# A hybrid attention, recurrence and mixture-of-experts block on one core: scores a step ahead, earlier splits, own tiles for raw weights, a gate spread by DMA

## Chip, cores and metric

One core of a Trainium2 chip runs the whole kernel as one launch. The metric is device time in microseconds (us), the median of several runs. TensorE is called PE, VectorE DVE, ScalarE ACT, GpSimd POOL and SyncE SP, as in the profile.

## The reference, cut to what matters

One layer on 512 latent tokens of width 1024 and 256 context tokens, all in float32. Two branches read the same projection; their outputs are lifted, gated and projected; a mixture of experts follows (32 experts, two per token).

```python
h  = ada_rmsnorm(x, g_mix, sh1, sc1);  hc = ada_rmsnorm(ctx, g_mix, mod_c[0], mod_c[1])
proj = h @ w_in;  proj_c = hc @ w_in[:, :CTX_COLS]
o_att = neighbourhood_attention(q, k, v, k_c, v_c, rpb)       # 8 heads of 64, window 8 x 16, plus all context keys
o_lru = (h_f + h_b) * gelu(proj[..., LG_OFF:...])             # conv, then scans in both directions, 1024 channels
y = sigmoid(proj_ga) * (o_att @ w_up_attn) + sigmoid(proj_gb) * (o_lru @ w_up_lru)
x = x + ga1 * (y @ w_out)
h2 = ada_rmsnorm(x, g_ffn, sh2, sc2)
x = x + ga2 * hier_moe(h2, ...)                               # top group, top-2 experts, SwiGLU 1024 -> 512 -> 1024
return rms(x) * g_final
```

## The kernel before

Most products are made exact to float32 by splitting both factors into a high and a low part and adding three products (`mm3`, L47). `wsplit` (L52) does this for a block of weights: SP loads the raw block, ACT copies it to a high part, DVE subtracts to get the low part. Raw and low tiles take turns in one ring of four buffers, `wlo`; the high tiles have a ring of three, `whi`. `next_weights` (L322) keeps two blocks in hand in the order that `weights_in_order` (L299) writes out.

A planner with a simulated clock (`schedule_with_timeline_sim`) lays out each engine's queue; `high_priority` and `issue_after` steer it, and `queued()` with `tail` ties the products of PE to the order of the program. Each engine then works through its queue in order.

The stages are:

- A prologue normalises x and the context, makes the first modulation and the values of attention.
- Four head pairs, j = 0 to 3 (L635). A pair is `keys` (L363), `queries` (L379), two of `lru_x` (L453, a projection of 512 latent and 256 context columns and a convolution), then `attend` (L394). `attend` goes over four blocks b of 128 queries: scores of two heads into the two banks of `at`, softmax on DVE (L416) and ACT (L418, L420), transposes (L429), products with the values (L440). Between these it calls `between(n)`, which runs n steps of the generator `others(j)` (L615): gate projections (`gate`, L521, result to DRAM), recurrences (`lru_g`, L474) and GeLU gates (`lru_o`, L510). A projection has three steps, `lru_g` four.
- `mod2` (L530) makes the second modulation on the side: 4 groups of 8 steps, each a load on POOL's queue and a multiply-add on DVE (L544). At a group's end ones-products sum it in a bank of `at` (L547), and a bias row comes over POOL's queue (L553). `others` calls one step after each of its eight parts. The relative bias of attention is loaded on POOL's queue too (L601).
- After the last pair `high` (L570) splits the four attention and eight recurrent outputs into high and low parts; `lift` (L578) multiplies them with `ua` and `ul`, two lifts of attention ahead of the first of the recurrence. SBUF that the pairs held comes free, and loads of x2, of w_out and of the first expert weights start there.
- The output projection and the router (`outp`, L750), with the tokens of the first expert pair gathered by one-hot products (L819) after 40 small products (L857).
- Sixteen expert pairs (L1110). Each reads 12 blocks of 1 MB: 8 for gate and up (`gu`, L1078), 4 for down (`down`, L1088). A ring of 22 tiles and two early ones hold the blocks that SP loads ahead (L908). `act` (L972) is the SiLU product and its transposes; `combine` (L988) scales by the routing weight and `ga2` and adds to x2 by one-hot products. `rows` (L932) gathers the next pair's tokens on POOL's queue. At pair 0, ahead of its last gate and up block, the two early tiles are closed, their place goes to the tiles of `act` and `combine`, and `broadcast` (L1032) loads the one row of `ga2` on SP's queue and spreads it over 128 partitions by products with ones and copies (L1037, L1038).

Of the kernel before, what the change touches and what calls it, by code (L numbers as in the profile page):

```python
# [9 lines left out]
F32 = mybir.dt.float32  # L10
# [27 lines left out]
def tile_block(ctx: ExitStack, tc: tile.TileContext, A, out):  # L38
# [13 lines left out]
    def wsplit(src, shape):  # L52

        n = shape[0] * shape[1]
        raw = ws.tile([128, 1024], F32, name="wlo", bufs=4)
        SP.dma_start(raw[:, :n], src)
        lo = ws.tile([128, 1024], F32R, name="wlo", bufs=4)
        hi = ws.tile([128, 1024], F32R, name="whi", bufs=3)
        S.copy(hi[:, :n], raw[:, :n])  # L59
        V.tensor_tensor(lo[:, :n], raw[:, :n], hi[:, :n].bitcast(F32), op=ALU.subtract)  # L60
        pat = "p (a b) -> p a b"
        return hi[:, :n].rearrange(pat, a=shape[0]), lo[:, :n].rearrange(pat, a=shape[0])

    tail = [None]
# [47 lines left out]
    ob = [op.tile([128, T], F32, name="ob", bufs=13) for _ in range(12)]  # L112
    olru = ob[4:]
# [185 lines left out]
    def weights_in_order():  # L299
        for j in range(4):  # L300
# [4 lines left out]
            for i in range(2):  # L305
                yield A["wcol"][24 + 4 * j + 2 * i], (NK, 128)
                if j < 3:
                    yield A["wcol"][24 + 4 * j + 2 * i + 1], (NK, 128)
                    yield A["wcol"][16 + 2 * j + i], (NK, 128)
                else:  # L310
                    yield A["wcol"][16 + 2 * j + i], (NK, 128)
                    yield A["wcol"][24 + 4 * j + 2 * i + 1], (NK, 128)
# [81 lines left out]
    def attend(j, kr, kx, qr, qp, between):  # L394

        po = ps.tile([128, 4, 128], F32, name="po")
        for b in range(4):
            w0 = WIN[b]
            scs = [ps.tile([128, 512], F32, name="at", bufs=2) for z in range(2)]
            q = slice(128 * b, 128 * b + 128)  # L400
            Ps, pts = [], []
            with tc.high_priority():

                with queued():
                    for c0, qs, ks in ((0, qr, kr[:, :, 8 * w0:8 * w0 + 256]), (256, qp, kx)):
                        for n, (a, h) in enumerate(((0, 0), (1, 0), (0, 1))):
                            for z, hs in enumerate(HALF):
                                cs = slice(256 - c0, 512 - c0) if z else slice(c0, c0 + 256)
                                m = PE.matmul(scs[z][:, cs], qs[hs, a, q], ks[hs, h, :], start=(n == 0), stop=(n == 2))
                tail[0] = m.ins  # L410
                for z in range(2):
                    sc = scs[z]
                    P = p1.tile([128, 512], F32, name="P", bufs=2)
                    st = p1.tile([128, 8], F32, name="st", bufs=4)

                    V.tensor_tensor_reduce(out=sc, in0=sc, in1=bias[z], scale=-1.0, scalar=3.0e38, op0=ALU.add,  # L416
                                           op1=ALU.min, accum_out=st[:, 0:1])
                    S.activation(P, sc, AF.Exp, bias=st[:, 0:1], scale=-1.0, accum_out=st[:, 3:4])  # L418
                    V.reciprocal(st[:, 4:5], st[:, 3:4])
                    S.activation(P, P, AF.Copy, scale=st[:, 4:5])  # L420
                    Ps.append(P)
            load_bias(j, b + 1)
            between(3)
            for z in range(2):
# [8 lines left out]
                between(1)  # L433
            with tc.high_priority():
# [100 lines left out]
    def mod2_g(g):  # L535
# [11 lines left out]
        pm = ps.tile([128, 256], F32, name="at", bufs=2)  # L547
# [10 lines left out]
        else:  # L558
            mt = ps.tile([128, 2, 128], F32, name="pt")
# [50 lines left out]
    kq = {}  # L610
    for step in (keys(0, kq), queries(0, kq), lru_x(0), lru_x(1)):
        for _ in step:
            pass

    def others(j):  # L615

        for i in range(2):
            c = 2 * j + i
            yield from gate(4 * j + 2 * i)
            next(m2s, None)  # L620
            yield from lru_g(c)
            next(m2s, None)
            if c < 7:
                lru_w(c + 1)
            if j < 3:
                yield from gate(4 * j + 2 * i + 1)
                next(m2s, None)
                yield from lru_o(c)
            else:
                yield from lru_o(c)  # L630
                next(m2s, None)
                yield from gate(4 * j + 2 * i + 1)
            next(m2s, None)

    for j in range(4):  # L635
        rest = others(j)
# [5 lines left out]
        attend(j, **kq, between=between)  # L642
        for _ in rest:
            pass
        if j < 3:
            kq = {}
# [788 lines left out]
```

## Time and profile before

| | us |
|---|---|
| median of 3 runs | 1072.51 (1071.69 to 1074.51) |
| the profiled execution | 1068.22 |
| its span, first to last instruction | 1066.5 |
| PE busy | 1003.0 (94%) |
| DVE busy | 562.5 (53%) |
| ACT busy | 428.9 (40%) |
| moved by DMA | 293.89 MB, mean 276 GB/s |

A busy share is a mean over the whole span. The share in each stage, and what an engine waits for there, has to be read stage by stage. PE's granted clock has two levels here, 1.0 for 2.4 GHz and 0.5 for 1.2 GHz.

### The profile page before, as it was taken

What the parts mean: (1) busy time and instruction counts of PE and PEld (TensorE: products, weight loads), DVE (VectorE), ACT (ScalarE), POOL (GpSimd) and SP (SyncE); (2) the same over time, 40 slices, a digit from 0 to 9 for tenths busy, and PEclk for the clock granted to TensorE, in tenths of its full rate; (3) what the DMA queues carried; (4) which work ended last, traced back from release to release, by engine and by line L of the source; (5) the groups of instructions that cost most, each with busy time, mean ns of one, the idle gap of its engine ahead of it and who ended that gap; (6) DMA issues with size and microseconds to landing.
All of it is one profiled execution on the core that took longest, in us unless ns stands there. A gap on an engine that the chain in (4) does not pass through costs nothing.

```text
span 1066.5 us, 13848 instructions
## 1 busy us (share of the span) xinstructions
PE 1003.0 (94%) x5196; PEld 614.3 (58%) x5196; DVE 562.5 (53%) x1150; ACT 428.9 (40%) x762; POOL 95.1 (9%) x159
## 2 busy tenths in 40 slices
PE   8998989989998999889999799999999999989995
PEld 7787768767876866568787434444444344333332
DVE  5678559657865965767448423333333353322234
ACT  4334784776488377724122122222222222212204
POOL 0021011101101100211001300000000000000001
PEclk9999999999999999989999989999999999999998
DMA  9575235324423622385787979999999999999992
GB/s 372 194 253 173 95 135 175 116 98 158 138 91 119 205 92 79 114 315 191 263 328 279 385 274 420 420 421 420 420 420 421 420 420 419 421 420 421 422 398 97
DMA packets 59034, 293.89 MB, mean 276 GB/s; under 512 B 8705, under 2 KB 9241, under 8 KB 33364
## 3 DMA queue, kind: packets, MB, share of 16 engines
q1 hardware_dynamic: 43636, 252.45, 59.5%
q0 software_dynamic: 11856, 34.22, 9.6%
q10 hardware_dynamic: 3472, 6.30, 1.6%
q8 instruction: 42, 0.69, 0.3%
q14 instruction: 28, 0.23, 0.1%
HBM read 287.24 MB, written 9.65 MB: 278 GB/s over the span
## 4 chain that ended last, share of the span: by engine, by line
PE 58%; DMA 22%; ACT 9%; DVE 7%; issue 2%; SPq 0%; ACTq 0%; DVEq 0%
DMA w<-in_ew 16%; PE g L1084 13%; PE y L1097 7%; PE pj L48 7%; PE pj L49 6%; PE pj L50 6%; DMA wlo<-in_wcol 3%; PE pj L489 2%; PE pc L1003 2%; PE pc L1004 2%; DVE wlo L60 1%; PE po L759 1%; DMA wlo<-in_ua 1%; PE po L761 1%; PE po L760 1%
## 5 line engine op out<-in xcount | busy, mean ns | idle before, releaser
L1084 PE MATMUL g<-w,xg 128*64 128x512 f32 x1024 | 232.5, 598 | 5.5 <-DMA w<-in_ew 4.9
L1084 PEld LDWEIGHTS g<-w,xg 128*64 128x64 f32 x1024 | 68.3, 136 | 139.9 <-issue 119.7
L48 PE MATMUL pj<-hh,whi 128*128 128x512 f32 x320 | 131.5, 411 | 0.1
L49 PE MATMUL pj<-hl,whi 128*128 128x512 f32 x320 | 127.1, 397 | 0.0
L50 PE MATMUL pj<-hh,wlo 128*128 128x512 f32 x320 | 126.8, 396 | 0.0
L1097 PE MATMUL y<-w,hT 128*64 128x512 f32 x512 | 115.7, 601 | 5.8 <-DMA w<-in_ew 5.2
L947 ACT ACTIVATE xg<-pc,sh2col,s2col 128x128 f32<-128x128 f32 x120 | 45.1, 459 | 153.1 <-PE pc L944 153.1
L977 DVE TENSOR_TENSOR hm<-hm,g 128x512 f32<-128x512 f32 x16 | 11.0, 688 | 179.1 <-PE g L1084 165.8
L60 DVE TENSOR_TENSOR wlo<-wlo,whi 128x1024 fp32r<-128x1024 f32 (+1 forms) x60 | 69.0, 1151 | 46.0 <-ACT whi L59 45.8
L59 ACT CAST whi<-wlo 128x1024 fp32r<-128x1024 f32 (+1 forms) x60 | 59.4, 991 | 78.3 <-DMA wlo<-in_wcol 26.3
L1097 PEld LDWEIGHTS y<-w,hT 128*64 128x64 f32 x512 | 35.3, 139 | 82.8 <-issue 60.6
L994 DVE SCALAR_TENSOR_TENSOR hm<-y,stok,ga 128x512 f32<-128x512 f32 x31 | 23.3, 751 | 110.6 <-PE y L1097 110.6
L1006 DVE TENSOR_TENSOR x<-x,pc 128x512 f32<-128x512 f32 x122 | 75.6, 680 | 6.3 <-PE pc L1004 6.3
L995 ACT CAST y_h<-hm 128x512 fp32r<-128x512 f32 x31 | 19.2, 620 | 131.8 <-DVE hm L994 71.5
L48 PEld LDWEIGHTS pj<-hh,whi 128*128 128x128 f32 x320 | 60.4, 189 | 17.6 <-ACT tr L491 2.9
L50 PEld LDWEIGHTS pj<-hh,wlo 128*128 128x128 f32 x320 | 60.4, 189 | 14.7
L49 PEld LDWEIGHTS pj<-hl,whi 128*128 128x128 f32 x320 | 60.5, 189 | 12.1
L1003 PE MATMUL pc<-y_h,ot 128*128 128x512 f32 x122 | 51.3, 421 | 0.3 <-ACT xg L947 0.3
L489 PE MATMUL pj<-xc,ga 128*128 128x256 f32 (+1 forms) x128 | 49.7, 516 | 0.0
L934 POOL DMA_INDIRECT xr<-nd,toki x15 | 16.7, 1113 | 354.2 <-PE pc L981 271.3
L1004 PE MATMUL pc<-y_l,ot 128*128 128x512 f32 x122 | 48.0, 393 | 0.0
L49 PE MATMUL pj<-ob,whi 128*128 128x512 f32 x96 | 39.3, 409 | 5.2 <-DVE ob L575 5.2
(372 smaller groups left out, 1668.8 us busy)
## 6 DMA issues: line engine op xcount, KB each, us to landing
w<-in_ew SPq DMA_DIRECT2D x191, 1024.0 KB, 20.1
wlo<-in_wcol SPq DMA_DIRECT2D x40, 512.0 KB, 3.6
m<-in_wm POOLq DMA_DIRECT2D x32, 512.0 KB, 4.1
wm<-in_wm SPq DMA_DIRECT2D x8, 1024.0 KB, 11.8
bias<-in_rpb POOLq DMA_DIRECT2D x32, 128.0 KB, 2.4
gd<-ga ACTq DMA_DIRECT2D x16, 256.0 KB, 3.7
wlo<-in_ul SPq DMA_DIRECT2D x8, 512.0 KB, 3.4
ga<-gd POOLq DMA_DIRECT2D x16, 256.0 KB, 3.6
```

Source lines behind the costliest of these rows:

```text
L48: PE.matmul(o, wh, hh, start=start, stop=False)
L49: PE.matmul(o, wh, hl, start=False, stop=False)
L50: return PE.matmul(o, wl, hh, start=False, stop=stop)
L59: S.copy(hi[:, :n], raw[:, :n])
L60: V.tensor_tensor(lo[:, :n], raw[:, :n], hi[:, :n].bitcast(F32), op=ALU.subtract)
L489: m = PE.matmul(pg[:, 0:n], lw[:, 128 * w:128 * w + 128], xc[:, s0:s0 + n], start=True, stop=True)
L947: S.activation(xg[z][:, k % 4, :], pg[:, k % 4, :], AF.Identity, bias=sh2col[:, k:k + 1], scale=s2col[:, k:k + 1])
L1003: PE.matmul(pc, ot[:, i, :], y_h, start=True, stop=False)
L1004: m = PE.matmul(pc, ot[:, i, :], y_l, start=False, stop=True)
L1006: V.tensor_add(x2[:, i, ns], x2[:, i, ns], pc)
L1084: m = PE.matmul(pgu[pr][v][64 * e:64 * e + 64, :], xg[pr][k // 4][:, k % 4, 64 * e:64 * e + 64], w[:, v, e, :], start=(k == 0), stop=(k == ...
L1097: m = PE.matmul(py[64 * e:64 * e + 64, :], hT[:, k, 64 * e:64 * e + 64], w[:, k % 2, e, :], start=(k == 0), stop=(k == 3))
```

## The change

- **Scores a step ahead.** `attend` is cut in two. `scores(j, b)` holds the scores, the softmax and the load of the next bias; `attend` calls `scores(j, b + 1)` before the transposes of block b. Block 0's scores stand in `start(j)`, between the two `lru_x`. `P` has three buffers. The calls of `between` are 2, 1, 2, 1 instead of 3, 1, 1, 1.
- **Second modulation.** Its sums and transposes use the ring `pj` (four banks, those of the projections) instead of `at` and `pt`; `others` calls up to 12 steps per pair.
- **Branch outputs.** The attention output is split straight from PSUM into `oatt`. In pair 3 the order of `others` is new (both recurrences early, two gates last), and `high(c)` splits the recurrent outputs while the pair runs, into the tiles of the context's `hh` and `hl`, whose pool now lives as long as the lifts.
- **Raw weights.** While the lifts run, `wsplit` puts raw blocks into two tiles of their own.
- **Small steps later.** The router's constants and two index steps are issued after lift 10.
- **Experts.** `ga2` is spread by one DMA on POOL's queue. At pair 0, 34 products of 128 x 128 stand between the gate and up products and the activation.

```diff
-        raw = ws.tile([128, 1024], F32, name="wlo", bufs=4)
+        raw = (wraw[0] or ws).tile([128, 1024], F32, name="wraw" if wraw[0] else "wlo", bufs=2 if wraw[0] else 4)
...
+    hcp = R.enter_context(pool("hTc", "right"))
     r1 = R.enter_context(ExitStack())
-    hcp = r1.enter_context(pool("hTc", "right"))
...
-    ob = [op.tile([128, T], F32, name="ob", bufs=13) for _ in range(12)]
-    olru = ob[4:]
+    oatt = [[op.tile([128, T], F32R, name=f"oa{z}{j}") for z in range(2)] for j in range(4)]
+    olru = [op.tile([128, T], F32, name="ob", bufs=9) for _ in range(8)]
...
-    def attend(j, kr, kx, qr, qp, between):
+    def scores(j, b, kr, kx, qr, qp):
...
+                P = p1.tile([128, 512], F32, name="P", bufs=3)
...
+        load_bias(j, b + 1)
+        return Ps
+
+    def attend(j, kq, Ps, between):
         po = ps.tile([128, 4, 128], F32, name="po")
         for b in range(4):
...
-            load_bias(j, b + 1)
-            between(3)
+            between(2)
+            ahead_ = scores(j, b + 1, **kq) if b < 3 else None
+            pts = []
             for z in range(2):
...
-                between(1)
+                between(1 + z)
...
                 if b == 3:
-                    V.tensor_copy(ob[j].rearrange("p (r b c) -> p b r c", b=4, c=16),
-                                  po.rearrange("p b (r c) -> p b r c", c=16))
+                    pat = "p (r b c) -> p b r c"
+                    src = po.rearrange("p b (r c) -> p b r c", c=16)
+                    h, l = (o.rearrange(pat, b=4, c=16) for o in oatt[j])
+                    S.copy(h, src)
+                    V.tensor_sub(l, src, h.bitcast(F32))
             between(1)
+            Ps = ahead_
...
-        pm = ps.tile([128, 256], F32, name="at", bufs=2)
+        pm = ps.tile([128, 256], F32, name="pj", bufs=4)
...
-            mt = ps.tile([128, 2, 128], F32, name="pt")
+            mt = ps.tile([128, 2, 128], F32, name="pj", bufs=4)
...
-    def high(k, pl):
-
-        h = pl.tile([128, T], F32R, name=f"oh{k}")
-        l = op.tile([128, T], F32R, name="ob", bufs=13)
-        S.copy(h, ob[k])
-        V.tensor_sub(l, ob[k], h.bitcast(F32))
-        return h, l
+    def high(c):
+
+        if c % 4 == 0:
+            ohs.append(hcp.tile([128, NK, TC], F32R, name=("hch", "hcl")[c // 4]).rearrange(
+                "p (a b) t -> p a (b t)", b=2))
+        h = ohs[c // 4][:, c % 4, :]
+        l = op.tile([128, T], F32R, name="ob", bufs=9)
+        S.copy(h, olru[c])
+        V.tensor_sub(l, olru[c], h.bitcast(F32))
+        parts.append((h, l))
...
+    def start(j):
+
+        kq = {}
+        run(keys(j, kq))
+        run(queries(j, kq))
+        run(lru_x(2 * j))
+        Ps = scores(j, 0, **kq)
+        run(lru_x(2 * j + 1))
+        return kq, Ps
+
     def others(j):
...
+        g, c = 4 * j, 2 * j
+        if j < 3:
+            order = (gate(g), lru_g(c), gate(g + 1), lru_o(c), gate(g + 2), lru_g(c + 1), gate(g + 3), lru_o(c + 1))
+        else:
+            order = (gate(g), lru_g(c), gate(g + 1), lru_g(c + 1), lru_o(c), lru_o(c + 1), gate(g + 2), gate(g + 3))
+        for n, step in enumerate(order):
+            if n == 1 and c < 7:
+                lru_w(c + 1)
+            if n == 5 and j < 3:
+                lru_w(c + 2)
+            yield from step
             next(m2s, None)
+            if n % 2:
                 next(m2s, None)
+            if j == 3:
+
+                for k in ((0, 1), (2,), (3,), (4,), (5, 6), (7,), (), ())[n]:
+                    high(k)
...
     for j in range(4):
+        kq, Ps = start(j)
         rest = others(j)
...
+        attend(j, kq, Ps, between)
+        run(rest)
+    run(m2s)
...
-    oha = l2.enter_context(pool("oha"))
-    parts = [high(k, oha) for k in range(4)]
+    wraw[0] = l2.enter_context(pool("wraw"))
     tas = [lift(A["ua"][m], 4, 0, m) for m in range(2)]
...
-    with pool("ohl", "right") as ohl:
-        parts += [high(k, ohl) for k in range(4, 12)]
...
-    V.tensor_copy(sg[:, :, 4], pidx[:, 0:4])
+    with tc.issue_after(lifted[10]):
+        V.tensor_copy(sg[:, :, 4], pidx[:, 0:4])
...
-        cst = router_consts(nc, p3, ps3, A, s2col, sh2col, ones)
+        with tc.issue_after(lifted[10]):
+            cst = router_consts(nc, p3, ps3, A, s2col, sh2col, ones)
...
-                    broadcast(ga2, modd[3:4, :])
+                    G.dma_start(ga2, modd[3:4, :].to_broadcast([128, D]))
...
+            if pr == 0:
+
+                wu = ps4.tile([128, 128], F32, name="pc", bufs=4)
+                with queued():
+                    for _ in range(34):
+                        m = PE.matmul(wu, one, one, start=True, stop=True)
+                tail[0] = m.ins
             hT, after, pt = act(pgu[pr])
```

## Rows read from the trace of the kernel before

**Rows 1.** The page: DMA busy tenths in 40 slices of the span.

```profile
DMA  9575235324423622385787979999999999999992
```

**Rows 2.** Busy us (count) by stage: PE, PEld, DVE, ACT, POOL; clock, DMA share, GB/s.

```profile
64.90:444.70 379.80, 362.93 (x1989) 278.90 (x1988) 268.02 (x427) 247.68 (x382) 42.76 (x80) 0.99 0.40 131
444.70:515.00 70.30, 61.72 (x248) 48.51 (x247) 49.30 (x90) 23.98 (x50) 13.58 (x31) 0.93 0.70 251
...
596.00:632.00 36.00, 30.95 (x122) 11.37 (x124) 7.57 (x18) 9.28 (x20) 7.85 (x12) 0.86 0.77 296
632.00:920.00 288.00, 288.00 (x1348) 115.95 (x1348) 96.37 (x169) 69.55 (x143) 12.51 (x12) 1.00 1.01 419
920.00:1035.00 115.00, 104.89 (x458) 39.08 (x456) 33.63 (x54) 21.53 (x43) 2.24 (x2) 1.00 1.01 420
```

**Rows 3.** Chain that ended last from 800 us: start us, us, what.

```profile
818.55 19.81 DMA w<-in_ew
```

**Rows 4.** PE's waits, 64.9 to 444.7 us: who for whom, us in total, times, longest.

```profile
PE pt L429 <- ACT P L420: 15.6, 7, 4.1
PE po L440 <- ACT PT L432: 1.0, 2, 0.7
```

**Rows 5.** Busy us by window at the lower clock, columns as in rows 2.

```profile
107.80:111.30 3.50, 3.50 (x10) 2.16 (x9) 1.83 (x3) 2.11 (x5) 0.00 (x0) 0.51 0.42 157
...
449.10:456.00 6.90, 5.63 (x12) 3.97 (x13) 6.90 (x15) 1.71 (x3) 2.72 (x9) 0.51 0.91 322
466.20:469.70 3.50, 3.36 (x8) 2.64 (x9) 3.35 (x8) 1.60 (x6) 0.56 (x1) 0.51 0.97 372
```

**Rows 6.** PE's waits, 444.7 to 480 us.

```profile
PE pj L49 <- DVE ob L575: 5.2, 2, 4.5
PE pj L48 <- ACT whi L59: 2.5, 2, 2.2
PE pj L50 <- DVE wlo L60: 0.8, 1, 0.8
```

**Rows 7.** PE's time line: start us, us, instruction; first projection after lru_x(2j).

```profile
87.46 0.40 PE L48 MATMUL pj<-hh,whi 128*128 128x512 f32 x1
87.69 0.40 PE L49 MATMUL pj<-hl,whi 128*128 128x512 f32 x1
...
279.71 0.40 PE L48 MATMUL pj<-hh,whi 128*128 128x512 f32 x1
```

**Rows 8.** DVE's time line: the query's last step in pairs 0 and 2, a modulation step.

```profile
88.92 0.69 DVE L360 TENSOR_TENSOR qr<-rc,qr 128x512 fp32r<-128x512 f32 x1
...
273.80 1.27 DVE L544 SCALAR_TENSOR_TENSOR acc<-m,c,acc 128x1024 f32<-128x1024 f32 x1
...
283.54 0.68 DVE L360 TENSOR_TENSOR qr<-rc,qr 128x512 fp32r<-128x512 f32 x1
```

**Rows 9.** Chain that ended last, 430 to 520 us.

```profile
450.78 14.81 DMA wlo<-in_ua
```

**Rows 10.** DMA issues by line (400 to 520, 560 to 1066 us): count, KB, us to landing.

```profile
ga<-modd POOLq DMA_DIRECT2D x2, 256.0 KB, 16.0
...
xr<-nd,toki POOLq DMA_INDIRECT x15, 8.1
```

**Rows 11.** Busy us in a window of expert pair 0, columns as in rows 2.

```profile
616.70:624.40 7.70, 7.03 (x20) 2.22 (x20) 0.00 (x0) 2.25 (x4) 0.00 (x0) 0.57 0.08 20
```

**Rows 12.** Time line of PE at ga2's spread; chain: down products of pairs 0 and 1.

```profile
614.03 3.78 PE L1037 MATMUL pc<-ga,ones 1*128 1x512 f32 x4 [3.97 <-DMA ga<-modd]
...
619.53 8.92 PE y L1097 x32
...
651.30 6.87 PE y L1097 x32
```

**Rows 13.** Time line of PE: the 40 small products ahead of the experts.

```profile
587.21 2.39 PE L857 MATMUL pr<-one 128*128 128x128 bf16 x40 [0.40 <-DVE le L1340]
```

**Rows 14.** Waits of POOL's queue over the span: us in total, times, longest.

```profile
POOL bias L601 <- DVE st L416: 191.3, 15, 16.4
```

More of the change, by code (lines that the diff above doesn't have):

```diff
@@ L304, in weights_in_order @@
                 yield A["wcol"][8 + c], (NK, 128)
[L305 to L312, printed above, removed]
+            g, c = 24 + 4 * j, 16 + 2 * j
+            for n in (g, g + 1, c, g + 2, g + 3, c + 1) if j < 3 else (g, g + 1, c, c + 1, g + 2, g + 3):
+                yield A["wcol"][n], (NK, 128)
         yield A["ua"][0], (4, 128)
@@ L392, in queries @@
         yield from proj(next_weights(A["wcol"][4 + j]), 0, out)
-    def attend(j, kr, kx, qr, qp, between):
+    def scores(j, b, kr, kx, qr, qp):
+        w0 = WIN[b]
+        scs = [ps.tile([128, 512], F32, name="at", bufs=2) for z in range(2)]
+        q = slice(128 * b, 128 * b + 128)
+        Ps = []
+        with tc.high_priority():
+            with queued():
+                for c0, qs, ks in ((0, qr, kr[:, :, 8 * w0:8 * w0 + 256]), (256, qp, kx)):
+                    for n, (a, h) in enumerate(((0, 0), (1, 0), (0, 1))):
+                        for z, hs in enumerate(HALF):
+                            cs = slice(256 - c0, 512 - c0) if z else slice(c0, c0 + 256)
+                            m = PE.matmul(scs[z][:, cs], qs[hs, a, q], ks[hs, h, :], start=(n == 0), stop=(n == 2))
+            tail[0] = m.ins
+            for z in range(2):
+                sc = scs[z]
+                P = p1.tile([128, 512], F32, name="P", bufs=3)
+                st = p1.tile([128, 8], F32, name="st", bufs=4)
+                V.tensor_tensor_reduce(out=sc, in0=sc, in1=bias[z], scale=-1.0, scalar=3.0e38, op0=ALU.add,
+                                       op1=ALU.min, accum_out=st[:, 0:1])
+                S.activation(P, sc, AF.Exp, bias=st[:, 0:1], scale=-1.0, accum_out=st[:, 3:4])
+                V.reciprocal(st[:, 4:5], st[:, 3:4])
+                S.activation(P, P, AF.Copy, scale=st[:, 4:5])
+                Ps.append(P)
+        load_bias(j, b + 1)
+        return Ps
@@ L396, in attend @@
+    def attend(j, kq, Ps, between):
         po = ps.tile([128, 4, 128], F32, name="po")
         for b in range(4):
[L398 to L421, printed above, removed]
@@ L568, in tile_block @@
     lifted = []
-    def high(k, pl):
-        h = pl.tile([128, T], F32R, name=f"oh{k}")
-        l = op.tile([128, T], F32R, name="ob", bufs=13)
-        S.copy(h, ob[k])
-        V.tensor_sub(l, ob[k], h.bitcast(F32))
-        return h, l
+    def high(c):
[7 more added lines that the diff above has]
+        parts.append((h, l))
+    ohs = []
+    parts = [tuple(o) for o in oatt]
     def lift(src, n, k0, m):
@@ L609, in tile_block, with run @@
         G.dma_start(d, none)
-    kq = {}
-    for step in (keys(0, kq), queries(0, kq), lru_x(0), lru_x(1)):
+    def run(step):
         for _ in step:
             pass
-    def others(j):
-        for i in range(2):
-            c = 2 * j + i
-            yield from gate(4 * j + 2 * i)
-            next(m2s, None)
[L621 to L626, printed above, removed]
-                next(m2s, None)
[L628 to L633, printed above, removed]
+    def start(j):
[6 more added lines that the diff above has]
+        return kq, Ps
+    def others(j):
+        g, c = 4 * j, 2 * j
[9 more added lines that the diff above has]
+            yield from step
+            next(m2s, None)
+            if n % 2:
+                next(m2s, None)
+            if j == 3:
+                for k in ((0, 1), (2,), (3,), (4,), (5, 6), (7,), (), ())[n]:
+                    high(k)
     for j in range(4):
+        kq, Ps = start(j)
         rest = others(j)
@@ L640, in between @@
                 next(rest, None)
[L642 to L646, printed above, removed]
-            for step in (keys(j + 1, kq), queries(j + 1, kq), lru_x(2 * j + 2), lru_x(2 * j + 3)):
-                for _ in step:
-                    pass
-    for _ in m2s:
-        pass
+        attend(j, kq, Ps, between)
+        run(rest)
+    run(m2s)
     l1.close()
@@ L743, in tile_block @@
         xtp = xtx.enter_context(pool("xt"))
[L744 removed]
+        with tc.issue_after(lifted[10]):
+            cst = router_consts(nc, p3, ps3, A, s2col, sh2col, ones)
         cst["one"] = one
```

55 lines of the change are left out of this document (29 added, 26 removed).

## The prediction

> **What bounds the kernel now.** I read the page first, then the busy time by stage, then who waits for whom on PE inside the stages, and last the queues. The span has two halves with different limits. In the table by stage [rows 2] the four head pairs (64.9 to 444.7 us) keep PE busy 362.9 of 379.8 us with the DMA engines 40% used: PE's own queue is the bound there. From 632 us to 1035 us the DMA share is 1.01 at 419 to 420 GB/s: the stream of expert weights is the bound. The page's slices show the same change near slice 20 [rows 1]. PE is still full up to 920 us only because it lives on weights loaded ahead; after that it loses 115 - 104.9 = 10.1 us waiting for them, and the chain of waits is a row of weight loads of some 20 us each from 818 us on (six rows follow each other, the first is shown) [rows 3].
>
> So two things move the end: PE work ahead of the experts that finishes earlier, because the memory for the weights comes free when that work is done and the whole stream then starts earlier; and any hole in the stream once it runs. PE time saved inside the experts after the stream is full is worth nothing.
>
> **Part 1, scores a step ahead.** PE waits in the head pairs are 15.6 us for the softmax (seven waits) and 1.0 us for a copied transpose [rows 4], 16.6 us together, which is nearly all of the 16.9 us that PE idles there [rows 2]. Three of the waits are followed by a stretch of 3.5 us at a granted clock of 0.51, half speed, which costs about 3.5 x 0.49 = 1.7 us each (the first of the three is shown) [rows 5]: 5.1 us. Gross: 21.7 us. The cause is that scores and transposes lie one projection apart (`between(3)`), while the softmax's VectorE and ScalarE steps queue behind the recurrent scans. With the scores of the next block issued before this block's transposes, the softmax gets six steps of `others` instead of three, twice as long. I leave 2 us of these waits.
>
> The change adds a wait. Block 0's scores now stand after `lru_x(2j)` instead of after both, and need the rotated query. PE ends `lru_x(2j)` and starts the next projection at 87.46 us in pair 0 and at 279.71 us in pair 2 [rows 7], but VectorE finishes the query only at 88.92 + 0.69 = 89.6 and 283.54 + 0.68 = 284.2 us [rows 8]. Where the scores stand now, PE would idle 2.1 and 4.5 us; the two other pairs lie between, so about 13 us in all. Behind the waiting scores the whole PE queue stands, `lru_x(2j+1)` first. An idle stretch of 4 us brings half speed with it, so up to four times 1.7 us more: 19.8 us at most. At least it is nothing: the query is late because VectorE works off the second modulation in these stretches, each step 1.27 us, three of them in pair 2 between the key and the query (one is shown) [rows 8]. `others` now takes up to 12 modulation steps per pair instead of 8, so they should be over after pair 2 and spread into the attention, where VectorE has room. I take 2.1 and 2.4 us for pairs 0 and 1, 1 and 0.8 for 2 and 3, and one drop of the clock, 8 us, nearer the lower half since its cause can move. Net of part 1: 21.7 - 2 - 8, about 12 us; bounds 0 and 20.
>
> **Part 2, branch outputs split during the last pair.** At the end of the pairs PE idles 5.2 us for the split of the attention outputs, which stands on VectorE behind the last scans, then 2.5 + 0.8 us for the split of a lift's weights [rows 6], 8.5 us. Two stretches at 0.51 follow, of 5.63 and 3.36 busy us [rows 5]: 2.8 + 1.6 = 4.4 us. Gross 12.9 us. The new order of pair 3 ends with two gates, so the last scan and the GeLU products lie a good 10 us of PE work before the end (24 matmuls 0.23 us apart [rows 7], 5.6 us a gate), and `high` runs under it. The 5.2 us and the 2.8 us go: 8 us. The 16 casts and subtractions cost nothing as long as those two gates cover them; without the cover they are the 5.2 us again. Also, `oatt` is written straight from PSUM, one VectorE copy less per pair.
>
> **Part 3, raw weights in own tiles; router constants later.** What comes next is the weight wait of 2.5 + 0.8 us with its 1.6 us of half speed, 4.9 us. Its row is a load of only 256 KB that took 14.81 us [rows 9]: it was issued into a burst of x2, the first expert weights and w_out, and its slot had come free only when the previous lift's low half was made. With own raw tiles this load can leave before the burst. But the next one (`ul[1]`) has to wait for the split of `ul[0]`, whose high half takes the tile of the last gate's weights, so it leaves with the burst, and PE now arrives 8 us earlier. I keep 3.4 of the 4.9 us as lost (bounds 0 and 9), so parts 2 and 3 give 9.5 us net, bounds 4 and 13. Holding the constants back behind `lifted[10]` removes small VectorE steps from this stretch; they are needed only in the output stage, so it costs nothing.
>
> **Part 4, gate spread by a DMA, and warm products.** In expert pair 0 PE idles 3.97 us for the one-row load of ga2, then multiplies it out in 3.78 us, all at half speed; the down products take 8.92 us instead of the 6.87 us of the next pair [rows 12]. Without the broadcast PE is through the gate and up products at 614.03 - 3.97 = 610.1 us. The 34 warm products take 34/40 of 2.39 us [rows 13], 2.0 us, and lie over the activation that PE waits for anyway, at most 1 us of them on its path. The down products then start near 613.4 instead of 619.5 us and end near 620.3 instead of 628.4: 8 us for PE. What counts is the stream: from 616.7 to 624.4 us it stands at a share of 0.08, a hole of 7.7 x 0.92 = 7.1 us, since every slot is full until the down products free some [rows 11]. Now they come free in time for four chunks; then the stream needs the first slot of pair 1, and PE gets there only when the gathered rows (8.1 us to land) are turned and the spread gate has come. The spread moves 512 KB; the nearest rows are the gather of the same size, 8.1 us, and half of that size in the burst, 16.0 us [rows 10]. I take 8: it is just late and a hole of 2 us stays, bounds 0.5 and 4. The spread's bytes take 0.52 MB / 420 GB/s = 1.2 us of the stream [rows 2]. Net 7.1 - 2 - 1.2, about 4 us, bounds 2 and 6. On POOL's queue the new DMA stands by the gathers; nothing else is behind it.
>
> Here the Trainium skill has a rule against the change (DMA: Bandwidth & Descriptors, section "Issuing engines are not separate DMA queues"): issuing from another engine saves only the sequencer's time, since all transfers share the same 16 engines. The trace agrees as far as POOL's 256 KB took 16.0 us while SP's burst ran [rows 10]. By the rule alone part 4's DMA would be worth only the removed PE work, less its bytes, which is what the sum above has.
>
> **Memory and banks.** The context tiles now live on for the split outputs, in place of the pool that stood there, and the outputs take 8 KB more per partition. I cost this at nothing, since the weights' memory is still freed by the same lifts; if a chunk lost its early place it would be one load, 2.5 us at 420 GB/s [rows 2].
>
> **The sum.** 12 + 9.5 + 4 = 25.5 us. The profiled execution took 1068.22 us (span 1066.5), so it would take 1042.7; the median of the runs is 4.3 us above it, 1072.51, and less 25.5 that is 1047.0 us.
>
> **Rivals.** (a) Wait for wait: VectorE keeps its order, scores wait the full 19.8 us, part 1 gives about 0: 13.5 to 15 us in all, 1058 us. For it: the queries are late in every pair; against: the modulation moves. (b) Clean: no new wait, no burst: 20 + 13 + 6 = 39 us, near 1034 us. (c) The stream does not follow the front, because what frees its memory moved too: only part 4 stays, near 1069 us, which lies on the bound of no change and is counted there. Against: the ring was already full when PE came to it [rows 11]. (d) Slower: the modulation's sums now take turns in the projections' four PSUM banks. A bank is held until its bias row has come through POOL's queue, which stood behind VectorE's scores for up to 16.4 us at a time, 191.3 us over 15 waits [rows 14]. Next to `lru_g`, which turns over four banks in a few us, PE would then wait up to 14 us, plus 1.7 of half speed, at each of four sums. It turns the result where it exceeds 25.5 / 4, some 6.4 us, per sum; at 10 us each it is 1072.5 - 25.5 + 40 = 1087 us.
>
> **Chances.** Forecast (1039 to 1055 us) 0.48; (a) 0.24; (b) 0.17; (c) 0.05; (d) 0.06. The range takes in most of (a) and (b): 1034 to 1063 us. A measurement here tells 0.3%, 3.2 us, from no change: faster 0.89, same 0.05, slower 0.06.
>
> **What would show it.** Right: the waits for P gone from PE's list; scores waiting for the query by 2 us in pairs 0 and 1; no wait on split outputs after the last gate; no idle before the down products of pair 0; the stream's hole under 4 us; its end and the experts' start earlier by the same 21 us. Wrong: PE waiting at the sums of the modulation, a weight load of over 10 us at the second lift, or a front that is earlier while the stream is not.

## The result

The changed kernel is slower: 1087.51 us median (1084.12 to 1090.01, 4 runs) against 1072.1 us of the kernel before beside it, a ratio of 1.0139, 95% interval 1.0105 to 1.0173. The forecast was 1047.0 us, range 1034 to 1063 us. The profiled execution took 1088.48 us, its span is 1086.7 us.

The stages of the changed kernel, as [rows 2] of before (stretch and its length, then busy us and count of PE, PEld, DVE, ACT, POOL; granted clock, DMA share, GB/s): the four head pairs, the lifts, the output stage, then the entry of the experts in two pieces and the rest.

```profile
72.00:170.70 98.70, 91.07 (x498) 69.85 (x497) 67.10 (x103) 62.09 (x94) 14.23 (x26) 0.98 0.48 151
170.70:284.40 113.70, 96.87 (x509) 73.21 (x508) 78.98 (x119) 62.41 (x95) 14.04 (x26) 0.94 0.43 140
284.40:379.40 95.00, 89.41 (x497) 68.86 (x497) 65.40 (x100) 61.49 (x93) 8.62 (x16) 1.00 0.35 110
379.40:466.60 87.20, 83.59 (x465) 64.09 (x464) 60.88 (x99) 63.39 (x100) 4.84 (x9) 1.00 0.28 90
466.60:539.70 73.10, 67.90 (x289) 54.76 (x288) 38.87 (x76) 23.69 (x52) 12.43 (x29) 0.98 0.70 245
539.70:612.40 72.70, 68.05 (x406) 58.25 (x404) 48.89 (x236) 16.07 (x46) 7.49 (x8) 0.98 0.88 340
612.40:632.00 19.60, 18.89 (x114) 7.70 (x116) 1.55 (x6) 3.49 (x6) 6.29 (x11) 1.00 0.89 328
632.00:654.00 22.00, 10.24 (x40) 5.64 (x38) 6.24 (x13) 5.27 (x11) 2.08 (x2) 0.69 0.65 253
654.00:1040.00 386.00, 377.05 (x1744) 148.50 (x1740) 123.47 (x212) 90.04 (x184) 14.75 (x14) 1.00 1.01 417
```

The lifts, 80.9 us before, have shrunk to some 73 us as meant. Pair 1 has grown from 92.9 to 113.7 us, at a mean clock of 0.94, and is the largest loss; of its 113.7 us PE is busy for 96.9. And in the 22 us from 632 us on PE is busy for 10.2 us. The head pairs (70.5 to 444.7 us before, from the first product with the context on) take 394.6 us against 374.2; PE idles 33.7 us in them (length less PE's busy time) where it idled 16.9, and the half clock costs 8.5 us where it cost 5.1 (one less the granted clock, summed over windows of half a us): 16.8 + 3.4 = 20.2 of the 20.4 us that the pairs lost.

Who waits for whom on PE in the head pairs (us in total, times, longest), to be held against [rows 4]:

```profile
PE pt L433 <- DVE PT L436: 14.4, 6, 3.7
PE at L404 <- ACT qr L356: 6.7, 3, 5.1
PE pj L48 <- ACT gi L499: 4.0, 4, 1.6
PE pj L569 <- DVE m L562: 2.4, 1, 2.4
PE at L404 <- DVE qr L357: 2.1, 3, 0.8
PE pt L433 <- DVE st L414: 1.8, 3, 1.1
PE pj L497 <- ACT ga L533: 1.3, 1, 1.3
```

The waits for P are gone to the last one. In their place the transposes wait for the copy PT that empties the one `pt` bank (14.4 us), the scores for the rotated query (8.8 us), and the modulation's transposes for its sums (2.4 us). How the copy came late is on VectorE's time line in pair 1 (start us, us, instruction; some lines left out):

```profile
242.20 1.23 DVE L61 TENSOR_TENSOR wlo<-wlo,whi 128x1024 fp32r<-128x1024 f32 x1 [0.37 <-ACT whi L60]
243.34 0.69 DVE L411 CUSTOM_DVE_ANT_0 at<-at,bias 128x512 f32<-128x512 f32 x1
...
243.95 0.73 DVE L411 CUSTOM_DVE_ANT_0 at<-at,bias 128x512 f32<-128x512 f32 x1
...
244.60 1.28 DVE L552 SCALAR_TENSOR_TENSOR acc<-m,c,acc 128x1024 f32<-128x1024 f32 x1
245.80 0.68 DVE L524 SCALAR_TENSOR_TENSOR ga<-ga,pj 128x512 f32<-128x512 f32 x1
246.39 0.68 DVE L436 COPY PT<-pt 128x512 f32<-128x512 f32 x1
```

And on PE's, the two halves' transposes (lines between left out):

```profile
240.68 0.66 PE L433 MATMUL pt<-ident,P 128*128 128x128 f32 x4
...
247.13 0.67 PE L433 MATMUL pt<-ident,P 128*128 128x128 f32 x4 [3.70 <-DVE PT L436]
```

PE had done the first transposes by 241.3 us. Their copy begins at 246.39: a weight split, the softmax of the next block, a modulation step and a GeLU product stand ahead of it. The second transposes start at 247.13 after 3.70 us idle, and 3.4 us at half clock follow (247.6 to 251.1).

The entry of the experts: POOL's time line, then windows of 4 us (columns as above).

```profile
612.83 1.17 POOL L893 DMA_DIRECT2D s<-std  x2
613.96 0.99 POOL L902 MEMSET xr<- 128x1024 f32 x1
625.32 0.56 POOL L1135 DMA_DIRECT2D ga<-modd  x1 [10.37 <-issue]
625.86 3.20 POOL L893 DMA_DIRECT2D s<-std  x6
642.23 1.06 POOL L952 DMA_INDIRECT xr<-nd,toki  x1 [13.17 <-DVE y_l L1014]
```

```profile
638.00:642.00 4.00, 0.00 (x0) 0.00 (x0) 3.19 (x8) 0.62 (x1) 0.00 (x0) 0.77 1.02 426
642.00:646.00 4.00, 0.00 (x0) 0.00 (x0) 0.75 (x1) 0.00 (x0) 1.06 (x1) 0.50 0.83 321
646.00:650.00 4.00, 1.65 (x9) 1.65 (x9) 0.00 (x0) 1.58 (x3) 0.00 (x0) 0.50 0.02 8
650.00:654.00 4.00, 4.00 (x12) 2.69 (x12) 2.29 (x4) 3.07 (x9) 1.02 (x1) 0.52 0.17 37
654.00:658.00 4.00, 4.00 (x20) 1.26 (x18) 1.06 (x2) 1.17 (x2) 0.00 (x0) 1.00 0.38 109
```

ga2's DMA waits 10.37 us for the memory that the early tiles give back ahead of the last gate and up block, and six of the eight loads of the routing records stand behind it on POOL's queue. The records land late, then comes the list of tokens, then the gather: at 642.23 us, 29.8 us after the first gate and up product (613.75 us before, 17.6 us after it). PE, done with the down products, waits 11.8 us for those rows, and works at half clock until 653.9 us. The hole in the stream of weights is 4 x (0.17 + 0.98 + 0.83 + 0.62) = 10.4 us where it was 7.1 [rows 11].

### The profile page after: what moved, and what is told of

Read it like the earlier page. It is cut to its first block, busy times and chain, and to the rows that moved or that the text cites. A ratio compares the mean times of both kernels' runs of the same rounds, so it can differ in the third digit from the quotient of the medians.

```text
span 1086.7 us, 13890 instructions
## 1 busy us (share of the span) xinstructions
PE 1003.9 (92%) x5226; PEld 619.7 (57%) x5226; DVE 558.2 (51%) x1146; ACT 430.1 (40%) x760; POOL 95.9 (9%) x160
## 5 line engine op out<-in xcount | busy, mean ns | idle before, releaser
L1102 PEld LDWEIGHTS g<-w,xg 128*64 128x64 f32 x1024 | 68.2, 137 | 140.6 <-issue 119.6
L1115 PEld LDWEIGHTS y<-w,hT 128*64 128x64 f32 x512 | 34.9, 137 | 79.4 <-issue 60.0
L61 DVE TENSOR_TENSOR wlo<-wlo,whi 128x1024 fp32r<-128x1024 f32 (+1 forms) x45 | 54.3, 1206 | 47.4 <-ACT whi L60 47.3
L60 ACT CAST whi<-wlo 128x1024 fp32r<-128x1024 f32 (+1 forms) x45 | 46.6, 1035 | 56.5 <-DMA wlo<-in_wcol 37.3
L497 PE MATMUL pj<-xc,ga 128*128 128x256 f32 (+1 forms) x128 | 47.2, 510 | 1.5 <-ACT ga L533 1.3
L552 DVE SCALAR_TENSOR_TENSOR acc<-m,c,acc 128x1024 f32<-128x1024 f32 x28 | 35.8, 1277 | 11.3 <-DMA m<-in_wm 11.3
## 6 DMA issues: line engine op xcount, KB each, us to landing
w<-in_ew SPq DMA_DIRECT2D x191, 1024.0 KB, 19.8
```

The source lines that it names most:

```text
L497: m = PE.matmul(pg[:, 0:n], lw[:, 128 * w:128 * w + 128], xc[:, s0:s0 + n], start=True, stop=True)
L1102: m = PE.matmul(pgu[pr][v][64 * e:64 * e + 64, :], xg[pr][k // 4][:, k % 4, 64 * e:64 * e + 64], w[:, v, e, :], start=(k == 0), stop=(k == ...
L1115: m = PE.matmul(py[64 * e:64 * e + 64, :], hT[:, k, 64 * e:64 * e + 64], w[:, k % 2, e, :], start=(k == 0), stop=(k == 3))
```

## The experiments

Times as a ratio to the kernel before, run beside each. Stages are us of the profiled execution: the four head pairs, PE's idle time and the clock's loss in them, the lifts, and from the first gate/up to the end. A profiled execution can lie some us from its kernel's median (the kernel before 4.3 us under it, e2 3.6 under, e11 5.0 above), so stage differences of that size are read with care. The difference of two ratios is uncertain by some 3 to 4 us, by their intervals. In the kernels' names m is the second modulation.

| kernel | median us | ratio, 95% interval | pairs | idle | clock | lifts | experts |
|---|---|---|---|---|---|---|---|
| before | 1072.51 | 1 | 374.2 | 16.9 | 5.1 | 80.9 | 470.4 |
| after | 1087.51 | 1.0139 (1.0105 to 1.0173) | 394.6 | 33.7 | 8.5 | 73.3 | 474.3 |
| e1 scores undone | 1081.14 | 1.0084 (1.0055 to 1.0114) | 392.3 | 29.2 | 11.9 | 69.5 | 473.0 |
| e2 pace undone | 1085.23 | 1.0127 (1.0100 to 1.0154) | 389.5 | 29.9 | 6.8 | 72.0 | 474.3 |
| e3 ga2 by SP | 1084.39 | 1.0126 (1.0094 to 1.0158) | 390.8 | 29.6 | 10.2 | 73.5 | 472.2 |
| e4 transposes first | 1088.24 | 1.0151 (1.0120 to 1.0182) | 394.7 | 32.6 | 10.2 | 73.7 | 473.5 |
| e5 e3, list first | 1075.55 | 1.0057 (1.0037 to 1.0076) | 392.6 | 28.9 | 11.9 | 73.1 | 464.4 |
| e6 parts 2, 3 | 1062.15 | 0.9913 (0.9887 to 0.9939) | 379.8 | 23.1 | 5.1 | 65.3 | 468.7 |
| e7 e6 + gate of e5 | 1054.83 | 0.9854 (0.9829 to 0.9879) | 376.3 | 21.8 | 1.7 | 65.3 | 464.4 |
| e8 e7 + scores ahead | 1066.88 | 0.9972 (0.9941 to 1.0003) | 383.1 | 25.9 | 5.1 | 72.4 | 464.4 |
| e9 e8, block 0 late | 1058.22 | 0.9883 (0.9862 to 0.9903) | 377.9 | 19.8 | 5.1 | 71.3 | 463.1 |
| e10 e7 + m's banks | 1075.80 | 1.0044 (1.0023 to 1.0064) | 399.3 | 34.9 | 13.7 | 65.4 | 464.9 |
| e11 e7 + m's pace | 1064.62 | 0.9947 (0.9924 to 0.9970) | 386.1 | 24.5 | 10.2 | 69.5 | 465.7 |
| e12 e9 + sums in pj | 1069.16 | 0.9986 (0.9972 to 1.0000) | 388.0 | 25.1 | 8.5 | 70.4 | 464.4 |
| e13 e10, m's transposes later | 1063.02 | 0.9917 (0.9890 to 0.9945) | 387.0 | 26.7 | 8.5 | 65.6 | 465.7 |
| e14 e7 + sums in pj | 1065.51 | 0.9950 (0.9932 to 0.9969) | 388.4 | 25.7 | 10.2 | 68.2 | 465.1 |
| e15 e7, old raw tiles | 1061.49 | 0.9929 (0.9900 to 0.9958) | 379.5 | 20.8 | 6.8 | 70.4 | 467.7 |

**e1, part 1 undone in the changed kernel.**

```
-        Ps = scores(j, 0, **kq)              # in start(j)
-            between(2)
-            ahead_ = scores(j, b + 1, **kq) if b < 3 else None
+            Ps = scores(j, b, **kq)
+            between(3)
```

> The changed kernel with part 1 taken back alone: a block's scores stand again right before its own transposes, three steps of other work between them, and block 0's scores after both lru_x. Theory 1 (the time was lost in the head pairs, because the scores put ahead stand with their softmax in front of the transposes' copy on VectorE and in front of a late rotated query): the waits for PT (14.4 us in four pairs) and for qr (8.8 us) vanish, waits for P come back (about 15 us), pair 1 goes from 113.8 to 93 to 98 us, and the total to 1066 to 1074 us. Theory 2 (the faster pace of the second modulation, 12 steps a pair instead of 8, and its sums in the projections' banks, is what pair 1 pays): pair 1 stays above 108 us and the total at 1083 to 1090 us.

Neither: 0.6% comes back, the waits for P are there again (17.4 us), and pair 1 still takes 104.7 us. Scores ahead is a part of the loss, not the whole.

**e2, the modulation's pace undone.**

```
             next(m2s, None)
-            if n % 2:
-                next(m2s, None)
```

> The changed kernel with the second modulation again at one step per step of the other work, 8 a pair instead of 12; its sums stay in the projections' banks, scores stay ahead. Theory 2 (the pace costs pair 1 its time): pair 1 falls from 113.8 to 95 to 100 us, pair 3 gets 2 to 4 us longer, the total is 1072 to 1077 us. Theory 1 (order on VectorE, whatever the modulation's pace): the waits for PT stay at 10 us or more over the pairs, the wait for the query appears in pairs 2 and 3 as well, and the total stays within 4 us of 1087.5 us.

Theory 2 fails in the total and is half true in pair 1, which falls to 104.3 us where it said 95 to 100. Pair 2 rises from 95.0 to 99.3 us: the transposes of the modulation now wait 3.1 us in each of the two. The total cannot be told from the changed kernel's, as theory 1 had it; the loss mostly moves with the modulation.

**e3, ga2's DMA on another queue.**

```
-                    G.dma_start(ga2, modd[3:4, :].to_broadcast([128, D]))
+                    SP.dma_start(ga2, modd[3:4, :].to_broadcast([128, D]))
```

> The changed kernel with one letter changed: the DMA that spreads ga2 is issued on SP's queue instead of POOL's, so that on POOL's queue the six last routing records and the row gather no longer stand behind it. Theory 3 (the records were held there until gate/up block 6 had freed the memory): the gather is issued some 13 to 25 us earlier, before 630 us, PE's wait of 11.8 us for the rows before pair 1's turn shrinks below 2 us, no half clock at 640 to 654 us, and the stretch from the first gate/up to the end shrinks by 4 to 9 us: 1079 to 1083 us. Rival (the stream of weights sets the end there, whatever PE waits): PE's wait goes and the total stays within 2 us of 1087.5 us.

Theory 3 does not hold in full: the records are all issued by 614 us, yet the gather leaves only at 632.14, PE still waits 9.7 us for the rows, and the total cannot be told from the changed kernel's. VectorE's time line of e3 shows the second half of the cause:

```profile
623.12 0.81 DVE L894 TENSOR_REDUCE stok<-s 128x48 f32<-128x384 f32 x1
623.96 0.18 DVE L898 TENSOR_SCALAR stok<-stok 128x16 f32<-128x16 f32 x1
629.53 0.75 DVE L1012 SCALAR_TENSOR_TENSOR hm<-y,stok,ga 128x512 f32<-128x512 f32 x1 [5.39 <-DMA ga<-modd]
630.20 0.17 DVE L899 TENSOR_SCALAR s<-stok 128x16 f32<-128x16 f32 x1
...
631.07 0.17 DVE L900 TENSOR_TENSOR toki<-s,stok 128x16 int32<-128x16 f32 x1
```

The planner put the first multiplication by ga2 ahead of the last two steps of the token list. VectorE stands there 5.39 us until ga2 lands, and the list, two steps of 0.17 us that need nothing of ga2, waits with it.

**e4, the first transposes ahead of the next scores.**

```
-            ahead_ = scores(j, b + 1, **kq) if b < 3 else None
             pts = []
+                if z == 0:
+                    ahead_ = scores(j, b + 1, **kq) if b < 3 else None
```

> The changed kernel with one step moved: the first half's transposes (z = 0) and their copy on VectorE are issued ahead of the next block's scores instead of behind them; the softmax is still a block ahead. Theory 1a (the copy out of the one pt bank queues on VectorE behind the softmax of the block just put ahead): the waits for PT, 14.4 us, fall below 4 us, the waits for qr (8.8 us) stay, the head pairs together shrink by 10 to 16 us, the total is 1071 to 1078 us. Rival (the copy is late because of the scans and splits that stand on VectorE in any case): the waits for PT stay at 10 us or more and the total within 4 us of 1087.5 us.

Neither in full: the waits for PT fall from 14.4 to 8.6 us, not below 4, and 5.2 us of waits of `lru_g` for its bank and a longer one for m (3.1 us) take their place. The total is the rival's. Moving this one step did not help.

**e5, e3 with the token list first.**

```
-        V.tensor_tensor(toki, tokx, stok[:, :, 0], op=ALU.add)
+        listed = [V.tensor_tensor(toki, tokx, stok[:, :, 0], op=ALU.add).ins]
+            with tc.issue_after(listed.pop()) if listed else nullcontext():
                 V.scalar_tensor_tensor(yv, py, gate, ga2[:, ns], op0=ALU.mult, op1=ALU.mult)
```

> The changed kernel with ga2's DMA on SP's queue as in e3, and on VectorE the first multiplication by ga2 held behind the token list (toki) that the row gather needs. In e3 the list stood behind that multiplication, which waited 5.4 us for ga2 to land. Theory 3b (the order on VectorE, after the order on POOL, is what makes the rows late): the gather is issued 6 to 8 us earlier against the end of gate/up than in e3, PE's wait of 9.7 us for the rows falls below 4 us, and first gate/up to the end goes from 472.2 us (e3) to 466 to 470 us; total 1078 to 1082 us. Rival (the gather is late for the normalized rows in memory, not the list): the wait stays at 8 us or more and the total within 2 us of e3, 1084.4 us.

Theory 3b holds, by more than it said: PE's wait for the rows falls to 1.9 us, and from the first gate/up to the end it takes 464.4 us, less than the 470.4 us of before. Against the changed kernel 0.0139 - 0.0057 = 0.8%, 9 us, came back by the order on two queues alone.

**e6 and e7, parts 2 and 3 alone, then with part 4 in the order of e5.** Scores as in e1; the modulation as before:

```
-        pm = ps.tile([128, 256], F32, name="pj", bufs=4)
+        pm = ps.tile([128, 256], F32, name="at", bufs=2)
-            mt = ps.tile([128, 2, 128], F32, name="pj", bufs=4)
+            mt = ps.tile([128, 2, 128], F32, name="pt")
```

> Parts 2 and 3 alone: the outputs split during the last pair, own raw tiles, router constants later; scores, the modulation's pace and banks, and ga2 as before the change. Theory (parts 2 and 3 bring what was forecast, 9.5 us, and the loss is all in the other parts): head pairs within 3 us of 374.3 us, lifts 70 to 74 instead of 80.9 us, total 1060 to 1065 us. Rival (the memory that the split outputs take delays the stream, so nothing arrives at the end): lifts shorter, total within 3 us of before, 1068 to 1074 us.

> Parts 2 and 3 with part 4 in the order of e5 (ga2 by SP's queue, token list first); scores and modulation as before. Theory (part 4's fault was only the order, its mechanism is sound): 1 to 6 us less than e6, 1056 to 1062 us. Rival (the spread's own landing, some 9 us in the stream, eats the gain): within 2 us of e6.

Both theories hold in the total. e6 is 9.3 us faster than before (0.0087 x 1071); its lifts gave more than expected and its pairs lost 5.6 us, 5.3 of it in pair 3 (93.7 against 88.4 us), whose order is new. In e7 the hole in the stream is 1.2 us and another 6.3 us are gained, 4.3 of them from the first gate/up on; the pairs, which part 4 does not touch, are 3.5 us shorter, 3.4 of it by fewer drops of the clock. e7 holds the 34 products too; no run separates them from the DMA. e7 is the fastest kernel of all: 1054.83 us, 1.5% under the kernel before.

**e8 and e9, scores ahead on top of e7.** e8 takes `scores` and `attend` as the change has them; e9 then moves one line:

```
-        Ps = scores(j, 0, **kq)
         run(lru_x(2 * j + 1))
+        Ps = scores(j, 0, **kq)
```

> The kernel of e7 with the scores put ahead as the change has them: all of the change but the modulation's pace and banks, gate in the order of e5. Theory 1 (scores ahead costs by VectorE's order even without the modulation's new pace): head pairs 378 to 386 us against 374 of e7, waits for qr and PT in place of those for P, total 4 to 12 us above e7. Theory 2 (all of the loss in the pairs was the modulation's, and scores ahead gains once it is back): head pairs 355 to 366 us, total 8 to 18 us below e7, near 1045 us.

> The kernel of e8 with one line moved: block 0's scores stand behind both lru_x again, the other blocks stay a block ahead. Theory (what scores ahead costs in e8 is the rotated query, 10.0 us of waits in the four pairs with the half clock behind them): the waits for qr vanish, head pairs fall from 383.1 to 369 to 375 us, total 1052 to 1058 us, level with e7. Rival (the query's wait only moves on, to the wait for P of block 0, since its softmax now has two steps less): head pairs stay above 379 us, total above 1061 us.

e8 loses 0.0118 x 1071 = 12.6 us on e7, as theory 1 had it. PE's waits in its pairs:

```profile
PE at L404 <- ACT qr L356: 8.6, 4, 3.6
PE at L557 <- ACT P L413: 5.3, 3, 2.0
PE pj L48 <- ACT gi L499: 4.0, 4, 1.5
PE pt L433 <- DVE PT L436: 2.9, 1, 2.9
PE pt L433 <- DVE st L414: 1.9, 3, 1.1
PE at L404 <- DVE qr L357: 1.4, 3, 0.8
```

Query 10.0 us, and 5.3 us for the modulation's sums, which need an `at` bank that the softmax of the block ahead now holds. e9 takes the query's wait away and 9.5 us come back (the pairs shrink by 5.2), so its theory holds in the main. It is still 3.1 us over e7, with intervals that overlap: its pairs idle 2 us less than e7's, but 4.8 us of waits for an `at` bank come up at block 1, whose scores need the banks that block 0's softmax still holds, and the lifts take 71.3 against 65.3 us, at a clock of 1.00 all through. There the load of the second lift's weights leaves 4.6 us ahead of the first lift, where it left 9.9 us ahead in e7, and PE waits 2.9 us for splits (whi). Why that load leaves later with the scores ahead was not tested.

**e10, e11, e13, e14, the modulation's edits on top of e7.** e10 has the two `pj` lines of the change, e11 its `if n % 2` line, e14 only the line of `pm`. e13 is e10 with a `yield` between sums and transposes (and one fewer among the loads).

> The kernel of e7 with the modulation's sums and transposes in the projections' four banks as the change has them, at the old pace of 8 steps a pair. Theory 2a (the bank is what the modulation's part costs: the transposes can now be issued right behind the sums and wait 3 to 4 us for VectorE, twice, with half speed behind each): head pairs 9 to 13 us longer than the 376.4 us of e7, total 1063 to 1068 us. Rival 2b (the pace is what costs): head pairs within 3 us of e7, total 1053 to 1058 us.

> The kernel of e7 with the modulation at 12 steps a pair as the change has it, its sums and transposes in the old banks. Theory 2a (the bank costs): head pairs within 4 us of e7's 376.4 us, total 1053 to 1059 us. Rival 2b (the pace costs, by 12 instead of 8 steps of 1.27 us on VectorE among the key and query steps and the softmax): pair 1 at 100 us or more against 92.5 us, head pairs 386 us or more, total 1064 us or more.

> The kernel of e10 (modulation in the projections' banks, old pace) with the two transposes of a modulation row issued one step of other work behind its sums instead of right behind them. Theory 2c (half of what the banks cost is that PE stands at these transposes, 2 x 4.06 us and the half clock behind them): the waits for m fall below 1 us together, head pairs 387 to 391 us against 399.3 us, total 1063 to 1068 us. Rival 2d (holding a projections' bank costs, wherever the transposes stand, because the projections then turn over three banks): head pairs stay above 395 us, total above 1071 us.

> The kernel of e10 with the transposes back in their old bank: only the modulation's sums stand in the projections' banks, old pace, scores as before. Theory 2c (the transposes cost): head pairs within 5 us of e7's 376.4 us, total 1054 to 1060 us. Rival 2d (the sums in a projections' bank cost): head pairs 386 us or more, total 1064 us or more.

Both cost: the banks 0.0190 x 1071 = 20.3 us, twice what theory 2a expected, and the pace 10.0 us, as rival 2b had it. In e10 PE issues the transposes right behind the sums. PE's line, then VectorE's:

```profile
261.25 0.64 PE L556 MATMUL pj<-acc,ones 128*32 128x256 f32 x8
265.95 0.44 PE L568 MATMUL pj<-ident,m 128*128 128x128 f32 x2 [4.06 <-DVE m L561]
```

```profile
261.18 1.26 DVE L512 TENSOR_TENSOR_SCAN w<-a,w 128x256 f32<-128x256 f32 x2
262.38 1.28 DVE L513 TENSOR_TENSOR_SCAN w<-a,w 128x512 f32<-128x512 f32 x1
...
263.57 1.26 DVE L513 TENSOR_TENSOR_SCAN w<-a,w 128x512 f32<-128x512 f32 x1
264.87 0.69 DVE L514 TENSOR_TENSOR ob<-w 128x512 f32<-128x512 f32 x1
265.48 0.42 DVE L561 TENSOR_TENSOR m<-pj,m 128x256 f32<-128x256 f32 x1
```

The sum's addition stands behind the recurrent scans. With sums in `at` and transposes in `pt` (before), the transposes came 14 us after the sums (242.86 and 256.93 us) and waited for nothing. e13 gives 0.0127 x 1071 = 13.6 us of the 20.3 back; e14, with no transposes there, still costs 10.3 us over e7. Both theories are true in part: the place of the transposes costs, sums in the projections' banks cost also, and the two do not add up to 20.3. The waits for P grow as well: 16.2 us in e7, 22.9 in e10, 20.8 in e14. In e14's profiled execution the pairs idle 3.9 us more than in e7 and lose 8.5 us more to the clock. But that execution is among the longest of e14's eleven. At mean clocks that both kernels had, 0.987 and 0.988, e14's runs take 1064.0 to 1065.0 us and e7's 1054.1 to 1056.5: the loss is there at the same mean clock. Why the order that the planner makes with these banks costs it is open.

**e12, e9 with the sums in `pj`.**

> The kernel of e9 with the modulation's sums in the projections' banks, its transposes in the old one. Theory (in e8 the sums waited 5.3 us because the at banks are now held by the softmax of the block ahead; the projections' banks are free of that): the waits at the sums vanish, head pairs 3 to 8 us shorter than in e9, total 1046 to 1054 us, faster than e7. Rival (the sums then wait for the projections' banks, or the time goes to other waits): head pairs within 2 us of e9 or longer.

The rival holds: no wait at the sums any more, but 7.1 us for PT and 7.2 us at `at`, and 11 us slower than e9. The sums in `pj` cost much the same with scores ahead as without (10.3 us, e14).

**e15, own raw tiles undone on top of e7.**

```
-    wraw[0] = l2.enter_context(pool("wraw"))
```

> The kernel of e7 with part 3's own raw tiles taken back: a lift's raw weights share their tiles with the low halves again. If the own tiles are worth what the forecast put on them, 1.5 us kept of 4.9 us, the lifts take 66 to 68 us instead of 65.3 us and the total is 1055 to 1058 us. Rival (they carry most of the lifts' gain of 15.6 us against the kernel before): lifts 72 us or more, total 1060 us or more.

Between the two: lifts 70.4 us, 5.1 more than in e7, with waits of 2.3 and 0.5 us for a weight's split back and one drop of the clock, total 0.0075 x 1071 = 8.0 us over e7.

## Why the prediction was wrong, step by step

From before to after the runs make a chain that adds up (each difference of ratios x 1071): parts 2 and 3 -9.3 (e6), part 4 in a good order -6.3 (e7), scores ahead +12.6 (e8), the modulation's pace and banks on top of that +9.1 (e5), part 4's order +8.8 (after): +14.9 us. The forecast was -9.5, -4, -12, 0 and 0. The largest miss is scores ahead: 24.6 us between -12 and +12.6.

- **What bounds the kernel**: right. PE's order bounds the pairs, and from 654 us the stream runs at 1.01. Time lost ahead of the experts came through to the end.
- **Part 1, gross gain**: the mechanism held, the waits for P went. The step that failed is "I leave 2 us of these waits". What took their place was left at nothing: the transposes' waits for the copy PT out of their one bank (14.4 us in the changed kernel, 0.2 in the one before), the bank of `at` held a block longer (5.3 us in e8), and lifts 7 us longer. PE idled 25.9 us in e8's pairs, against 21.8 in e7's.
- **Part 1, the wait for the query**: the place was right, the term too small. VectorE's time line gave about 13 us [rows 7, 8], the sum took 6.3 of them, and 10.0 us came in e8. In the changed kernel it is 8.8 us, 5.7 of it in pair 1, where 2.4 was taken, with 6.8 us of half clock behind it; none in pair 3, where the modulation is over, as argued.
- **The modulation**: the sum had it for nothing and even as help to the query. The runs show +20.3 us by the banks alone, +10.0 by the pace alone, +9.1 for both once the scores are ahead. Rival (d) had the symptom (PE waits at the modulation, in `pj`), with the wrong cause: not POOL's bias row holds the bank, but the addition stands behind the scans on VectorE and the transposes right behind the sums on PE (e10, and in the changed kernel the sums at 274.04, the addition at 276.57, the transposes at 277.04 us). That its price, 1087 us, is the time measured is chance: it took 10 us of waiting at each of four sums, and in the changed kernel PE waits 0.6 us at the sums and 2.4 us at the transposes behind them.
- **Parts 2 and 3**: right in total, 9.3 us for 9.5, and partly by luck. The split outputs are covered, as said: PE does not idle in e6's lifts. The terms inside were off: own raw tiles were put at 1.5 us and brought 8.0 (e15), and the lifts gave 15.6 us in e6, of which the pairs lost 5.6 again and the output stage 3.3 (73.8 us for 70.5).
- **Part 4**: the mechanism was right, and its size near: in e7 the hole is 1.2 us, and 4.3 us of the 6.3 lie in the experts, for 4 forecast. In the changed kernel the down products of pair 0 take 7.09 us, 8.92 before, as said. The step that failed is "On POOL's queue the new DMA stands by the gathers; nothing else is behind it". Six record loads and through them the first gather were behind it. And the added wait for ga2's landing on VectorE was not followed to who is queued there: the token list. e3 mended one, e5 both.

On the cited rule (the Trainium skill, DMA: Bandwidth & Descriptors, section "Issuing engines are not separate DMA queues"): in e3 another issuing engine alone brings nothing that can be told, 1.0126 against 1.0139, intervals overlapping. That does not go against the rule, but it is no test of it either, since VectorE's order held the rows there. What the issuing queue did to the case was not bandwidth but order. The Trainium skill's page PSUM — Partial Sum Buffer, section "Engine vs sequencer instructions", says that the queues of ScalarE, VectorE and GpSimd are strictly first in, first out. For POOL and VectorE the traces agree: six record loads stood behind ga2's DMA for its 10.37 us, and e3's list steps of 0.17 us behind a 5.39 us wait.

## What to carry to other kernels

Where a planner lays out the queues, a DMA in place of computed work is priced by an assumed landing: list for each engine what the planner put behind the instruction that waits for it, and pin the order of the few steps that others wait for (the token list: 9 us for one pinned instruction and one changed queue). Moving work ahead does not take it off an in-order engine; price it by what it now stands in front of there, and by the bank it holds longer. A temporary that moves to another ring of banks also moves in the order: look where its consumer lands.

## What was not expected of the hardware

A wait of the same length brought the half clock in one kernel and not in another: e7's transposes idle 2.63 us before 233.49 us and the clock stays at 1.00 (first row); e10's idle 2.63 us before 335.36 us and 3 us at 0.53 go with it (second row); in the changed kernel 2.37 us before 277.04 were enough (third).

```profile
233.50:240.00 6.50, 6.21 (x37) 4.18 (x38) 2.56 (x4) 4.55 (x7) 0.00 (x0) 1.00 0.38 127
```

```profile
335.30:338.30 3.00, 2.94 (x10) 2.50 (x11) 1.50 (x3) 0.62 (x2) 0.00 (x0) 0.53 0.36 145
```

```profile
278.40:281.80 3.40, 3.40 (x10) 2.62 (x9) 2.24 (x5) 0.00 (x0) 0.17 (x1) 0.50 0.85 295
```

The kernel before shows it by itself: of its waits of 2.67, 2.67 and 2.68 us (before 138.64, 231.87 and 324.89 us) the first and the third go with 3.4 us at half clock, the second with none. So a drop cannot be put down to one wait by its length, and a small change of order can be worth up to 1.7 us more or less at each.

Nor is a lower clock all time lost. Between e14's runs at a mean clock of 0.980 and 0.990 lie 4.5 us (1068.33 and 1063.87), where one less the granted clock, summed as in the table, would make some 10.6 us; between e15's at 0.975 and 0.989 lie 12.0 us where it would make some 14.9. So the table's clock column gives at these two kernels more than the drops cost.
